# A two-layer trunk on one Trainium2 core: second shift and scale as whole matrix products on TensorE's column groups, and the convolution read from SBUF with two of its eight blocks on ScalarE and GpSimd

## The chip, the core and the metric

One core of one Trainium2 chip runs the whole program. The metric is device microseconds of one execution, median of three runs. TensorE is called PE, VectorE DVE, ScalarE ACT, GpSimd POOL, SyncE SP.

## What is computed

256 tokens of 2048 features pass through two layers. A conditioning vector `c` gives, for each layer, six vectors of 2048: shift, scale and gate for the mixer, shift, scale and gate for the MLP.

```python
c_act = silu(c)
for l in range(2):
    mod = c_act @ ada_w[l] + ada_b[l]              # [2048] @ [2048, 12288]
    shift1, scale1, gate1, shift2, scale2, gate2 = split(mod, 6)
    h = rms(x, norm1_g[l]) * (1 + scale1) + shift1
    mix = even_mixer(h) if l % 2 == 0 else attention(h)
    x = x + gate1 * mix
    h = rms(x, norm2_g[l]) * (1 + scale2) + shift2
    x = x + gate2 * (square(relu(h @ mlp_w1[l])) @ mlp_w2[l])
```

The even mixer projects h to u, v, a, g (1024 columns each). Mixer A gates gelu(u) with a causal 128-token mix of gelu(v). Mixer B takes y = a * sigmoid(g), a causal depthwise convolution of 31 taps over the 256 tokens for each of 1024 channels, a LayerNorm over channels and silu. Both go side by side into one output projection `ab_w_out`. Everything is float32.

## The kernel before

Weights come from HBM in tiles of 1 MiB, each 512 rows of K by 512 columns (or, for conditioning, 128 rows by 2048 columns). SP issues these loads in one queue, in program order, into a ring of four buffers, `raw` (`wraw`, L111); the input projection's tiles go into the three `wh` buffers instead. Products are done in one of two ways:

- The even mixer's input projection is in plain float32 (`gemm32`, L144): per weight tile eight matmuls of 128x128 stationary and 128x512 moving. There are 32 such tiles, 12 in the four quarters at the start and 20 after them.
- All else is split into a high and a low part (`wtile`, L124; the split is ACT's L94 and DVE's L95) and takes three fast matmuls for one (L183 to L185): 24 per tile. The output projection has 16 tiles, the MLP of a layer 128.

The scale and shift of the mixer and of the MLP are needed with features on the partitions ("columns"), the gates the same in every partition ("rows"). Either is a product of one vector with a 16 MiB matrix, and before the change DVE does nearly all of it: each weight is multiplied by its c and added to an accumulator of 128 partitions, and only the 128 partial sums go through PE. The work is cut into steps of one 1 MiB weight load each, kept in a queue (`ada_more`) and released by `side_work` (L134), so many steps per weight tile of the main products.

In the even mixer, from the point where `setup_even` is called:

- The row of gate 1 (`ada_row(0, 2)`, 16 steps and a finish) goes by ACT, which multiplies, and POOL, which adds (L302, L303).
- The columns of shift 2 and scale 2 (indices 3 and 4) go in quarters of 512 features (`ada_quarters(0, 3)`, 32 steps; L267, L269). The first quarter, 8 steps, is shared by ACT and POOL (L263, L265), the other three, 24 steps, are DVE's. The rates are 1.2, 2.5 and 0.8 steps per weight tile, so that the last steps run beside the first MLP tiles. `norm_start` needs only a quarter to be complete before the MLP's features of that quarter are made.
- The convolution is 8 blocks of 128 channels by 31 taps. Each block's padded input is copied to a PSUM bank (`yp`, L537), and every tap is one DVE instruction on 128x256 that reads that bank and the sum in SBUF (L540, L542). Ten taps are issued per weight tile, the rest before `layer_norm`.
- The output projection starts three of its four column chunks with mixer A's rows (six tiles; the third chunk's sums lie in the two `ms` banks) before mixer B's rows, which need `layer_norm`, enter.

A tile framework orders the instructions of each engine from this program; each engine then runs its own list in order, and waits at an instruction whose inputs are not there.

The lines that the prediction names: L153 the float32 matmuls, L183 to L185 and L210 to L212 the split ones, L94 and L95 the split, L107 transposes, L263, L265, L267, L269 the quarters, L302 and L303 gate 1, L297 the second layer-0 gate on DVE, L540 and L542 the taps, L607 and L616 the sums of `layer_norm`, L796 and L797 scores of the odd layer.

Of the kernel before, what the change touches and what calls it, by code (L numbers as in the profile page):

```python
# [36 lines left out]
R0, R1, R2, R4 = 1.2, 0.8, 0.75, 0.4  # L37
RA, NA = 2.5, 4
# [4 lines left out]
class Trunk:  # L43
    def __init__(self, ctx, tc, t):
# [12 lines left out]
        self.ms = pool("ms", 2, space=bass.MemoryType.PSUM)  # L57
# [4 lines left out]
        self.first = 0  # tiles still to be split by GpSimd  # L62
        self.conv_rate = 10
        self.conv_y = {}
        self.quarters = {}

# [1 line left out]
    def rsqrt(self, out, v):  # L68
        """out = v ** -0.5 for v > 0: a first guess from the bits, a third-order step, a Newton step."""
# [14 lines left out]
        # out <- 8/3 of its third-order step, then Newton with the 8/3 taken out again  # L84
# [7 lines left out]
    def split(self, src, hi, lo, engine=None):  # L92
        """src = hi + lo, both with the 12 significant bits that one pass of the array takes."""
        self.nc.scalar.copy(hi, src)  # L94
        (engine or self.nc.vector).tensor_tensor(lo, src, hi.bitcast(F32), op=ALU.subtract)  # L95
# [6 lines left out]
    def transpose4(self, srcs):  # L102
        """Up to four [128, n] blocks -> one PSUM bank, transposed side by side."""
        ps = self.tr.tile([P, 512], F32, tag="tr", name="trp")
        for i, s in enumerate(srcs):
            w = s.shape[-1]
            self.nc.tensor.transpose(ps[:w, i * P : i * P + s.shape[0]], s, self.ident[: s.shape[0], : s.shape[0]])  # L107
        return ps

# [14 lines left out]
    def wtile(self, w, k0, nk, n0, nw):  # L124
# [3 lines left out]
        # VectorE is busy with the norm when a phase's first tiles come: GpSimd splits those  # L128
# [6 lines left out]
    def side_work(self, size=1.0):  # L135
        """Work that is spread beside the weight tiles: conditioning and the convolution."""
# [7 lines left out]
        for _ in range(min(self.conv_rate, len(self.conv_queue))):  # L144
            self.conv_queue.pop(0)()
# [79 lines left out]
    def ada_col(self, layer, j):  # L225
        """self.mod[layer, j] = [128, 16], feature-major."""
# [19 lines left out]
    def ada_quarters(self, layer, j0, side=None, aided=0):  # L246
        """Columns j0 and j0 + 1 side by side, complete for 512 features after every eight steps.
        The first aided quarters go by ScalarE and GpSimd, with room for products in side."""
# [3 lines left out]
        def step(q, g, i):  # L252
# [6 lines left out]
            for k in range(4):  # L259
                c = self.cT[:, 4 * g + k : 4 * g + k + 1]  # L260
                if q < aided:
                    prod = acc if g + k == 0 else side[:, D + k * 512 : D + (k + 1) * 512]
                    nc.scalar.activation(prod, raw[:, k, :], AF.Copy, scale=c)  # L263
                    if g + k:
                        nc.gpsimd.tensor_tensor(acc, acc, prod, op=ALU.add)  # L265
                elif g + k == 0:
# [11 lines left out]
    def ada_row(self, layer, j, side=None):  # L278
        """self.mod[layer, j] = [128, 2048], the same in every partition. With side = [128, 4096],
        the products go to ScalarE and the sums to GpSimd."""  # L280
# [3 lines left out]
        def step(kb):  # L284
            raw = self.wraw(self.t["ada_w"][layer], kb, 1, j * D, D)
            if kb == 0:
                if side is None:
                    acc = self.tmp.tile([P, D], F32, tag="acc", name="acc", bufs=1)
                else:
                    acc = side[:, :D]  # L290
                box["acc"] = acc
# [6 lines left out]
            else:  # L298
                for i in range(2):
                    sl = slice(i * 1024, (i + 1) * 1024)  # L300
                    prod = side[:, D + i * 1024 : D + (i + 1) * 1024]
# [16 lines left out]
    def at_end(self, last):  # L318
        """Before the last product of a stage: no more work beside it."""
# [3 lines left out]
    def ada_more(self, rate, *lists):  # L323
        """Steps to be worked off beside the coming weight tiles, rate steps to a tile."""
# [26 lines left out]
    def norm_t(self, h, q, r):  # L351
        """Four blocks of (x * r).T in PSUM."""
# [4 lines left out]
    def norm_start(self, layer, which):  # L357
        """A function that gives 512 features' (shift, gain) columns: modulate(rms(x) * g) = x * rstd * gain + shift."""
# [14 lines left out]
    def norm_quarter(self, quarter, q, pair):  # L373
        """512 features of h.T, as (hi, lo)."""
# [10 lines left out]
    def norm_mod(self, layer, which):  # L385
        """h.T (hi, lo) of modulate(rms(x) * g, shift, scale)."""
# [6 lines left out]
    def gated(self, src, gate, h, c):  # L393
        """x[:, chunk] += gate * src, for one half"""
# [6 lines left out]
    def residual(self, ps, gate, c, last, part=None):  # L401
        """x[:, chunk] += gate * (ps + part)"""
# [621 lines left out]
```

## Time and profile before

| | |
|---|---|
| three runs | 2189.92, 2189.74, 2189.75 us; median 2189.75 |
| the profiled execution, first to last instruction | 2185.9 us |
| PE busy | 2090.9 us, 96% |
| DVE, ACT, POOL busy | 1564.9, 932.3, 146.7 us |
| bytes moved | 567.70 MB, mean 260 GB/s |
| granted PE clock, mean | 0.987 |

The profile is of one execution; its own time is not given apart, but the three runs lie 3.8 to 4.0 us above its span, and that much is taken to lie around the span. Times in the profile count from the first instruction. Busy PE is not PE at its peak: matmuls overlap, their ends are modelled, and the clock can be granted at less than full speed; so beside the busy time one reads how many matmuls start in a stretch, and the granted clock. Engines that are late matter only where PE waits for them.

### The profile page before, as it was taken

The page shows a single profiled execution, that of the slowest core. Times are in us where ns is not written, and L with a number is a line of the kernel's source. Part 1 is how long each engine was busy: PE and PEld are TensorE (multiplying, and loading weights), DVE is VectorE, ACT ScalarE, POOL GpSimd, SP SyncE. Part 2 cuts the span into 40 slices and gives each one's busy share as a digit, 9 for nine tenths or more (in the row PEclk, how much of TensorE's full clock was granted, in tenths as well). Part 3 has the DMA queues.
Part 4 walks back from the last instruction along what each step waited for, and adds up shares of the span by engine and source line. Part 5 has one row for each costly group of instructions (what it writes and reads, how often), then busy time and mean ns, then how long its engine had stood idle before and what let it go on. Part 6 is the DMA issues. An engine that isn't in the chain of part 4 may idle for free.

```text
span 2185.9 us, 23655 instructions
## 1 busy us (share of the span) xinstructions
PE 2090.9 (96%) x9138; PEld 1635.7 (75%) x9138; DVE 1564.9 (72%) x1763; ACT 932.3 (43%) x1184; POOL 146.7 (7%) x95
## 2 busy tenths in 40 slices
PE   2889999899999999999998999989999999999999
PEld 1444458678888888888888787868888888888887
DVE  6849999888777878787767878766656545554555
ACT  2135435444444334333436776444434433433432
POOL 0038710000000000000001000010000000000000
PEclk9999999899999999999999999989999999999999
DMA  9999968899898899989755646647778556556653
GB/s 350 384 346 330 332 242 295 275 317 339 315 337 315 329 326 319 339 304 334 270 174 174 211 158 214 229 154 250 256 271 264 178 192 189 189 192 192 189 191 122
DMA packets 238620, 567.70 MB, mean 260 GB/s; under 512 B 9150, under 2 KB 17784, under 8 KB 221864
## 3 DMA queue, kind: packets, MB, share of 16 engines
q1 hardware_dynamic: 236288, 562.60, 74.3%
q10 hardware_dynamic: 1564, 2.28, 0.3%
q8 instruction: 72, 1.18, 0.2%
q0 software_dynamic: 656, 1.31, 0.2%
q14 instruction: 40, 0.33, 0.0%
HBM read 564.06 MB, written 2.10 MB: 259 GB/s over the span
## 4 chain that ended last, share of the span: by engine, by line
PE 85%; DVE 9%; DMA 5%; ACT 1%; issue 1%; SPq 0%; ACTq 0%; DVEq 0%
PE mm L183 23%; PE mm L184 23%; PE mm L185 23%; PE mm L153 4%; DMA raw<-in_ada_w 4%; PE trp L107 3%; DVE accq L269 2%; DVE cvsq L542 1%; DVE wl L95 1%; PE mm L210 1%; PE mm L211 1%; PE mm L212 1%; PE sc L797 1%; PE sc L796 1%; DMA raw<-in_mlp_w 1%
## 5 line engine op out<-in xcount | busy, mean ns | idle before, releaser
L95 DVE TENSOR_TENSOR wl<-raw,wh 128x2048 fp32r<-128x2048 f32 (+2 forms) x312 | 704.7, 2259 | 424.0 <-PE mm L184 317.9
L94 ACT CAST wh<-raw 128x2048 fp32r<-128x2048 f32 (+3 forms) x316 | 596.6, 1888 | 774.1 <-PE mm L185 515.2
L183 PE MATMUL mm<-wh,f_h 128*128 128x512 f32 x1024 | 399.6, 390 | 0.0
L185 PE MATMUL mm<-wh,f_l 128*128 128x512 f32 x1024 | 399.3, 390 | 0.0
L184 PE MATMUL mm<-wl,f_h 128*128 128x512 f32 x1024 | 398.7, 389 | 0.0
L185 PE MATMUL mm<-wh,h_l 128*128 128x512 f32 (+2 forms) x928 | 358.2, 386 | 0.0
L183 PE MATMUL mm<-wh,h_h 128*128 128x512 f32 (+2 forms) x928 | 358.2, 386 | 0.0
L184 PE MATMUL mm<-wl,h_h 128*128 128x512 f32 (+2 forms) x928 | 357.0, 385 | 0.6 <-DVE wl L95 0.6
L185 PEld LDWEIGHTS mm<-wh,f_l 128*128 128x128 f32 x1024 | 192.2, 188 | 39.8
L184 PEld LDWEIGHTS mm<-wl,f_h 128*128 128x128 f32 x1024 | 192.3, 188 | 39.6
L183 PEld LDWEIGHTS mm<-wh,f_h 128*128 128x128 f32 x1024 | 192.3, 188 | 39.2
L184 PEld LDWEIGHTS mm<-wl,h_h 128*128 128x128 f32 x928 | 175.0, 189 | 34.0 <-DVE wl L95 1.1
L185 PEld LDWEIGHTS mm<-wh,h_l 128*128 128x128 f32 x928 | 174.9, 188 | 33.4
L183 PEld LDWEIGHTS mm<-wh,h_h 128*128 128x128 f32 x928 | 175.0, 189 | 32.7
L153 PE MATMUL mm<-raw,x 128*128 128x512 f32 x448 | 195.7, 596 | 1.0 <-ACT x L500 0.6
L269 DVE SCALAR_TENSOR_TENSOR accq<-raw,cT,accq 128x512 f32<-128x512 f32 x210 | 153.7, 749 | 16.6 <-DMA raw<-in_ada_w 13.3
L153 PEld LDWEIGHTS mm<-raw,x 128*128 128x128 f32 x448 | 84.6, 191 | 104.6 <-issue 98.5
L237 DVE SCALAR_TENSOR_TENSOR acc<-raw,cT,acc 128x2048 f32<-128x2048 f32 x60 | 140.8, 2346 | 9.7 <-DMA raw<-in_ada_w 9.7
L297 DVE SCALAR_TENSOR_TENSOR acc<-raw,cT,acc 128x2048 f32<-128x2048 f32 x48 | 112.7, 2347 | 4.4 <-DMA raw<-in_ada_w 4.4
L542 DVE SCALAR_TENSOR_TENSOR cvsq<-yp,convw,cvsq 128x256 f32<-128x256 f32 x240 | 96.0, 476 | 0.0
L303 POOL TENSOR_TENSOR side<-side 128x1024 f32<-128x1024 f32 x32 | 74.8, 2361 | 19.3 <-ACT side L302 19.3
L452 ACT ACTIVATE relu<-mm 128x512 f32<-128x512 f32 x60 | 35.8, 599 | 87.7 <-PE mm L185 81.5
(270 smaller groups left out, 2246.9 us busy)
## 6 DMA issues: line engine op xcount, KB each, us to landing
raw<-in_mlp_w SPq DMA_DIRECT2D x256, 1024.0 KB, 5.6
raw<-in_ada_w SPq DMA_DIRECT2D x192, 1024.0 KB, 5.4
raw<-in_ab_w_in SPq DMA_DIRECT2D x32, 1024.0 KB, 9.7
raw<-in_ab_w_out SPq DMA_DIRECT2D x16, 1024.0 KB, 8.3
raw<-in_mla_w_out SPq DMA_DIRECT2D x16, 1024.0 KB, 4.9
raw<-in_mla_w_ukv SPq DMA_DIRECT2D x8, 1024.0 KB
raw<-in_mla_w_uq SPq DMA_DIRECT2D x8, 768.0 KB, 4.8
raw<-in_mla_w_in SPq DMA_DIRECT2D x4, 1024.0 KB, 7.2
```

Of the source, the lines that this page charges most:

```text
L94: self.nc.scalar.copy(hi, src)
L95: (engine or self.nc.vector).tensor_tensor(lo, src, hi.bitcast(F32), op=ALU.subtract)
L107: self.nc.tensor.transpose(ps[:w, i * P : i * P + s.shape[0]], s, self.ident[: s.shape[0], : s.shape[0]])
L153: self.nc.tensor.matmul(ps[h], x[:, 4 * g + k, h * P : (h + 1) * P], raw[:, k, :], start=g + k == 0, stop=4 * g + k == KB - 1,)
L183: nc.tensor.matmul(o, a, hi[:, i, :nw], start=first, stop=False)
L184: nc.tensor.matmul(o, a, lo[:, i, :nw], start=False, stop=False)
L185: nc.tensor.matmul(o, b, hi[:, i, :nw], start=False, stop=last)
L237: nc.vector.scalar_tensor_tensor(acc, raw, self.cT[:, kb : kb + 1], acc, op0=ALU.mult, op1=ALU.add)
L269: self.last = nc.vector.scalar_tensor_tensor(acc, raw[:, k, :], c, acc, op0=ALU.mult, op1=ALU.add).ins
L297: nc.vector.scalar_tensor_tensor(acc, raw, c, acc, op0=ALU.mult, op1=ALU.add)
L303: nc.gpsimd.tensor_tensor(acc[:, sl], acc[:, sl], prod, op=ALU.add)
L542: nc.vector.scalar_tensor_tensor(o, y, wk, o, op0=ALU.mult, op1=ALU.add)
```

## The change

Four things are changed in the even mixer of layer 0; the rest of the program is the same but for names of PSUM buffers.

1. Shift 2 and scale 2 are no longer done in quarters. A new function, `ada_col_pe`, takes each 1 MiB step (128 rows of K by 2048 columns) as four float32 matmuls on PE. The stationary operand is one column of c, repeated 32 times; each matmul takes 512 of the 2048 columns as its moving operand and writes 32 partitions of one PSUM bank, `ms1`, so that the four lie in the four groups of 32 columns of the array. After 16 steps a copy on ACT and 16 small matmuls turn the four rows into columns with the bias.
2. The order: gate 1's steps alternate with those of shift 2, then come scale 2's, 49 steps in all at 1.5 per weight tile (`RB`). Nothing of it is left for the MLP.
3. The convolution: taps read the padded input in SBUF, and DVE's sums lie in PSUM (`ms0`, two blocks in one bank). Blocks 6 and 7 go by ACT, which multiplies both blocks' 128x256, and POOL, which adds 128x512 (`aided`). Eight DVE taps and two aided ones are issued per weight tile.
4. The `ms` banks being taken, the output projection starts two chunks with mixer A's rows (four tiles), not three.

```diff
-R0, R1, R2, R4 = 1.2, 0.8, 0.75, 0.4
-RA, NA = 2.5, 4
+RA, RB, R2, R4 = 8 / 3, 1.5, 0.75, 0.4
...
+    def ada_col_pe(self, layer, j):
...
+        def step(kb):
+            raw = self.wraw(self.t["ada_w"][layer], kb, 1, j * D, D)
+            if kb == 0:
+                box["acc"] = self.bank(1)
+            acc = box["acc"]
+            for s in range(4):
+                nc.tensor.matmul(
+                    acc[32 * s : 32 * s + 32], self.cT[:, kb : kb + 1].broadcast_to([P, 32]),
+                    raw[:, s * 512 : (s + 1) * 512], start=kb == 0, stop=kb == KB - 1,
+                )
+            if kb == KB - 1:
+                rows = self.tmp.tile([P, 512], F32, tag="t512", name="adar")
+                nc.scalar.copy(rows, acc)
...
+                for b in range(4):
+                    o = ps[:, 4 * b : 4 * b + 4]
+                    nc.tensor.matmul(o, rows[:, b * P : (b + 1) * P], firsts, start=True, stop=False)
+                    nc.tensor.matmul(o, self.ident, bias[:, b], start=False, stop=True)
...
-        g1, q34 = self.ada_row(layer, 2, side), self.ada_quarters(layer, 3, side, 1)
...
-        self.ada_more(R0, mixed)
-        self.ada_more(RA, q34[:NA])
-        self.ada_more(R1, q34[NA:])
+        g1 = self.ada_row(layer, 2, sq.rearrange("p a b -> p (a b)"))
+        s2 = self.ada_col_pe(layer, 3) + self.ada_col_pe(layer, 4)
+        mixed = [step for two in zip(g1[:16], s2) for step in two] + [g1[16]] + s2[16:]
+        self.ada_more(RB, mixed)
...
-                if k == 0:
-                    self.conv_y[b] = self.ms.tile([P, PAD + T], F32, tag="ms", name="yp")
-                    nc.scalar.copy(self.conv_y[b], ypad[:, b, :])
-                o, y, wk = cv[:, b, :], self.conv_y[b][:, k : k + T], self.convw[:, b, k : k + 1]
+                if k == 0 and b % 2 == 0:
+                    self.conv_acc[b // 2] = self.bank(0, (P, 2, T))
+                i, y, wk = self.conv_acc[b // 2][:, b % 2], ypad[:, b, k : k + T], self.convw[:, b, k : k + 1]
+                o = i if k < CONV_W - 1 else cv[:, b, :]
...
+            def aided(b, k):
+                prod = cv[:, b : b + 2, :] if k == 0 else self.tmp.tile([P, 2, T], F32, tag="t512", name="cvp")
+                for i in range(2):
+                    y, wk = ypad[:, b + i, k : k + T], self.convw[:, b + i, k : k + 1]
+                    if k == 0:
+                        nc.scalar.activation(prod[:, i], y, AF.Identity, bias=self.vecs[:, 64 + b + i : 65 + b + i], scale=wk)
+                    else:
+                        nc.scalar.activation(prod[:, i], y, AF.Copy, scale=wk)
+                if k:
+                    nc.gpsimd.tensor_tensor(cv[:, b : b + 2, :], cv[:, b : b + 2, :], prod, op=ALU.add)
...
+        self.conv_queue = [([], 8), ([], 2)]
...
-        pss = [self.psum2(), self.psum2(), [self.ms.tile([P, 512], F32, tag="ms", name=f"ms{h}") for h in range(NH)]]
+        pss = [self.psum2(), self.psum2()]
...
-            if c < 3:
+            if c < 2:
```

How this moves instructions, at three places. In the rows below, `raw`, `wh` and `wl` are weight buffers, `x0` the features, `cT` the columns of c, `mm` and `ms` PSUM banks, `trp` a bank for transposes; numbers tell one buffer from another; lines are those of the kernel that the row is from, L161 being L153 of before, L191 to L193 being L183 to L185, and L102 being L95.

PE's list in the last part of the input projection (the products of v and u), before:

```order
L153 MATMUL mm0_1151<-raw_1239,x0_117 128x512 x4
L153 MATMUL mm1_1152<-raw_1239,x0_117 128x512 x4
L107 MATMUL trp_1287<-ident_88,accq_762 128x128 x4
L153 MATMUL mm0_1273<-raw_1275,x0_117 128x512 x4
L153 MATMUL mm1_1274<-raw_1275,x0_117 128x512 x4
L153 MATMUL mm0_1273<-raw_1312,x0_117 128x512 x4
L153 MATMUL mm1_1274<-raw_1312,x0_117 128x512 x4
```

And in the changed kernel, in the same part:

```order
L291 MATMUL ms1_734<-raw_1191,cT_98 32x512 x4
L161 MATMUL mm0_1181<-raw_1183,x0_117 128x512 x4
L161 MATMUL mm1_1182<-raw_1183,x0_117 128x512 x4
L161 MATMUL mm0_1181<-raw_1221,x0_117 128x512 x4
L161 MATMUL mm1_1182<-raw_1221,x0_117 128x512 x4
L291 MATMUL ms1_734<-raw_1255,cT_98 32x512 x4
L161 MATMUL mm0_1181<-raw_1253,x0_117 128x512 x4
L161 MATMUL mm1_1182<-raw_1253,x0_117 128x512 x4
```

Before, PE's list holds nothing of a conditioning step but four transposes when a quarter ends; now a group of four L291 stands ahead of most weight tiles. In all there are 128 of them, in 34 unbroken runs, most of four, some of one, three or eight.

DVE's list where the input projection ends and the first output weights are split, before (`accq` are sums of the quarters, `mod_763` and `mod_764` finished columns):

```order
L542 SCALAR_TENSOR_TENSOR cvsq<-yp,convw,cvsq 128x256 x34
L95 TENSOR_TENSOR wl<-raw,wh 128x2048
L267 TENSOR_SCALAR accq<-raw,cT 128x512 x2
L269 SCALAR_TENSOR_TENSOR accq<-raw,cT,accq 128x512 x3
L221 TENSOR_REDUCE mod_764<-trp 128x4
L269 SCALAR_TENSOR_TENSOR accq<-raw,cT,accq 128x512
L223 TENSOR_TENSOR mod_764<-mod_764,ada_b 128x4
```

And in the changed kernel (`vu` holds v and u, `pm` the mixed v, `cat` the output projection's input):

```order
L615 SCALAR_TENSOR_TENSOR vu_852<-vu_852,rv_1153,sgug_672 128x128 x16
L566 SCALAR_TENSOR_TENSOR ms0_1303<-ypad_240,convw_647,ms0_1303 128x256 x16
L566 SCALAR_TENSOR_TENSOR cvsq_242<-ypad_240,convw_647,ms0_1303 128x256 x2
L102 TENSOR_TENSOR wl_1674<-raw_1671,wh_1673 128x2048
L635 SCALAR_TENSOR_TENSOR vu_852<-pm_1468,vecs_183,vu_852 128x128 x4
L102 TENSOR_TENSOR cat_l_1467<-trp_1477,cat_h_1466 128x4x128
```

After the norm of v (L615) 18 taps are left, where before 69 stood between it and the first split, and no conditioning step follows the split.

PE's list in the output projection where mixer A's rows of the second chunk end, before:

```order
L184 MATMUL mm1_1509<-wl_1740,cat_h_1440 128x512
L185 MATMUL mm1_1509<-wh_1739,cat_l_1441 128x512
L107 MATMUL trp_1792<-ident_88,accq_762 128x128 x4
L183 MATMUL ms0_1510<-wh_1782,cat_h_1440 128x512
L184 MATMUL ms0_1510<-wl_1783,cat_h_1440 128x512
```

And in the changed kernel:

```order
L192 MATMUL mm1_1535<-wl_1795,cat_h_1466 128x512
L193 MATMUL mm1_1535<-wh_1794,cat_l_1467 128x512
L291 MATMUL ms1_1679<-raw_1834,cT_98 32x512 x4
L291 MATMUL ms1_1679<-raw_1840,cT_98 32x512 x4
L191 MATMUL mm0_1532<-wh_1830,cat_h_1466 128x512
```

Before, a third chunk's two tiles of mixer A follow (into `ms0` and `ms1`); now two conditioning steps follow and then the first tile of mixer B's rows, into `mm0_1532`, the bank of chunk one.

More of the change, by code (lines that the diff above doesn't have):

```diff
@@ L62, in __init__, with bank, next_bank @@
         self.first = 0
-        self.conv_rate = 10
-        self.conv_y = {}
+        self.conv_acc = {}
+        self.turn = 0
         self.quarters = {}
+    def bank(self, i, shape=(P, 512)):
+        return self.ms.tile(list(shape), F32, tag=f"ms{i}", name=f"ms{i}")
+    def next_bank(self, shape=(P, 512)):
+        self.turn ^= 1
+        return self.bank(self.turn, shape)
     def rsqrt(self, out, v):
@@ L143, in side_work @@
             self.ada_queue.pop(0)[1]()
-        for _ in range(min(self.conv_rate, len(self.conv_queue))):
-            self.conv_queue.pop(0)()
+        for queue, rate in self.conv_queue:
+            for _ in range(min(rate, len(queue))):
+                queue.pop(0)()
     def gemm32(self, ps, x, w, g, n0):
@@ L244, in ada_col, with ada_quarters @@
         return [lambda kb=kb: step(kb) for kb in range(KB)]
-    def ada_quarters(self, layer, j0, side=None, aided=0):
+    def ada_quarters(self, layer, j0):
         nc = self.nc
@@ L260, in step @@
                 c = self.cT[:, 4 * g + k : 4 * g + k + 1]
[L261 to L266, printed above, removed]
+                if g + k == 0:
                     nc.vector.tensor_scalar(acc, raw[:, k, :], c, None, op0=ALU.mult)
@@ L276, in ada_quarters @@
         return [lambda q=q, g=g, i=i: step(q, g, i) for q in range(4) for g in range(4) for i in range(2)]
+    def ada_col_pe(self, layer, j):
+        nc = self.nc
+        box = {}
+        def step(kb):
[11 more added lines that the diff above has]
+                nc.scalar.copy(rows, acc)
+                ps = self.tr.tile([P, 512], F32, tag="tr", name="adac")
+                firsts = self.ident.rearrange("p (a b) -> p a b", b=32)[:, :, 0]
+                b0 = layer * 96 + j * KB
+                bias = self.ada_b[:, b0 : b0 + KB].rearrange("p (s b) -> p b s", b=4)
+                for b in range(4):
+                    o = ps[:, 4 * b : 4 * b + 4]
+                    nc.tensor.matmul(o, rows[:, b * P : (b + 1) * P], firsts, start=True, stop=False)
+                    nc.tensor.matmul(o, self.ident, bias[:, b], start=False, stop=True)
+                out = self.const.tile([P, KB], F32, tag=f"mod{layer}{j}", name=f"mod{layer}{j}")
+                nc.scalar.copy(out.rearrange("p (s b) -> p b s", b=4), ps[:, :KB].rearrange("p (b s) -> p b s", b=4))
+                self.mod[layer, j] = out
+        return [lambda kb=kb: step(kb) for kb in range(KB)]
     def ada_row(self, layer, j, side=None):
@@ L286, in step @@
             if kb == 0:
[L287 to L291, printed above, removed]
+                acc = box["acc"] = self.tmp.tile([P, D], F32, tag="acc", name="acc", bufs=1)
                 nc.gpsimd.memset(acc, 0.0)
@@ L427, in mlp @@
         self.hold = self.hold and layer > 0
-        started = [self.psum2(), self.psum2(), [self.ms.tile([P, 512], F32, tag="ms", name=f"ms{h}") for h in range(NH)]]
+        started = [self.psum2(), self.psum2(), [self.bank(h) for h in range(NH)]]
         for q in range(4 + AHEAD):
@@ L478, in even @@
         x = self.act.tile([P, KB, T], F32, tag="act", name="x0")
-        side = self.act.tile([P, 2 * D], F32, tag="act", name="side")
-        self.ada_more(8 / 3, self.ada_quarters(layer, 0))
+        self.ada_more(RA, self.ada_quarters(layer, 0))
         self.ada_steps(X_AT)
@@ L493, in even @@
         cv, sq = cvsq[:, 0], cvsq[:, 1]
-        pa, pg = self.psum2(), self.psum2()
-        pa1 = [self.ms.tile([P, 512], F32, tag="ms", name=f"pa1{h}") for h in range(NH)]
+        pa, pg, pa1 = self.psum2(), self.psum2(), [self.bank(h) for h in range(NH)]
         for q in range(4):
@@ L585, in even @@
                 )
-        self.ada_until(lambda: (layer, 2) in self.mod and self.quarters[layer, 3] >= 1)
         hh, hl = self.act_pair(KB, "cat")
@@ L822, in attend @@
             V = Vs[c % 3]
[L823 removed]
+            po = self.next_bank((P, 2, T))
             for i, pT in enumerate(pTs):
```

27 lines of the change are left out of this document (13 added, 14 removed).

## The prediction

> **What bounds the kernel now.** I read first the busy times of the engines on the page and the shares of the chain that ended last.
>
> ```profile
> PE 2090.9 (96%) x9138; PEld 1635.7 (75%) x9138; DVE 1564.9 (72%) x1763; ACT 932.3 (43%) x1184; POOL 146.7 (7%) x95
> PE 85%; DVE 9%; DMA 5%; ACT 1%; issue 1%; SPq 0%; ACTq 0%; DVEq 0%
> ```
>
> PE is the bound on the average. The change concerns one stretch, so the next view is the table by stretch: the last 20 input tiles (130 to 290), mixer A's end and the first output tiles (290 to 320), the output projection (to 410), the way into the MLP (to 430, with its first chunks to 510), and the MLP.
>
> ```profile
> core 0: us, PE busy (x) PEld busy (x) DVE busy (x) ACT busy (x) POOL busy (x), PEclk, DMA share, GB/s
> 130.00:290.00 160.00, 157.73 (x399) 71.51 (x400) 122.80 (x293) 80.66 (x108) 116.32 (x66) 1.00 0.90 325
> 290.00:320.00 30.00, 24.81 (x98) 16.99 (x97) 28.09 (x53) 9.10 (x12) 0.00 (x0) 0.83 0.66 230
> 320.00:410.00 90.00, 90.00 (x407) 74.30 (x406) 86.71 (x103) 40.67 (x41) 0.00 (x0) 1.00 0.85 297
> 410.00:430.00 20.00, 9.79 (x37) 7.49 (x36) 16.26 (x43) 9.14 (x19) 0.00 (x0) 0.66 0.79 263
> 430.00:510.00 80.00, 77.44 (x361) 62.68 (x360) 70.46 (x68) 36.80 (x45) 1.81 (x1) 1.00 0.86 294
> 510.00:1148.00 638.00, 638.00 (x2886) 527.33 (x2885) 493.41 (x319) 257.13 (x195) 4.36 (x6) 1.00 0.87 308
> ```
>
> In the columns of PE: it works 157.73 of 160 us, 90 of 90, 77.44 of 80 and 638 of 638, at full clock. What is put on PE's list in these stretches lengthens them, unless it falls into a hole; what is taken from DVE there gains only where PE waited for DVE. Counting also the part of the busy time that a clock below 1.00 took, the holes are:
>
> - 130 to 290: 160 - 157.73 = 2.3 us.
> - 290 to 320: 5.2 idle, and 24.81 x (1 - 0.83) = 4.2 by the clock, 9.4 us.
> - 410 to 430: 10.2 idle, and 9.79 x (1 - 0.66) = 3.3, 13.5 us.
> - 430 to 510: 2.6 us.
>
> In all 27.8 us, the most that relief of any other engine can return here. The chain of waits says whose the second hole is.
>
> ```profile
> 278.44 12.61 DVE cvsq L542 x33
> 291.05 0.24 issue
> 291.30 0.47 DVE cvsq L542
> 291.77 2.19 DVE wl L95
> 294.00 5.03 DMA raw<-in_ab_w_out
> 299.20 1.90 ACT wh L94
> 301.10 0.98 ACT vu L583 x2
> ```
>
> DVE works off its late taps until 291.8, only then splits the first output tile; that frees a `raw` buffer, the next load takes it, and ACT's cast of that load (L94) stands ahead of the gelu (L583) that mixer A's gate is made from.
>
> All sums below are differences to this execution's span of 2185.9 us; with the 3.85 us around it that is the median, 2189.75. A measurement of this kernel can tell about 0.2%, 4.4 us, from no change.
>
> **What is put on PE.** Thirty-two steps of four float32 matmuls, 128 in all, each with 512 moving columns. The kernel's other whole float32 matmuls give the price: the chain's one unbroken stretch of them, and the groups of L153's matmuls and weight loads.
>
> ```profile
> 188.17 53.23 PE mm L153 x124
> ```
>
> ```profile
> L153 PE MATMUL mm<-raw,x 128*128 128x512 f32 x448 | 195.7, 596 | 1.0 <-ACT x L500 0.6 <-DMA raw<-in_ab_w_in 0.4
> L153 PE MATMUL pa<-raw,x 128*128 128x512 f32 x64 | 32.0, 654 | 7.1 <-DMA raw<-in_ab_w_in 7.1
> L153 PEld LDWEIGHTS mm<-raw,x 128*128 128x128 f32 x448 | 84.6, 191 | 104.6 <-issue 98.5
> ```
>
> The program has 32 tiles x 8 = 256 such matmuls and the trace 448 + 64 = 512 records: each float32 matmul is two records. One record takes 53.23 / 124 = 0.429 us of PE. The moving columns are as many in L291, so its 256 records cost 0.429 each, if they run by themselves; that only 32 columns of the array are used saves nothing by this row. What matters is how many run at once, and no matmul of the kernel before uses column groups. So there are three cases.
>
> - One after another: 256 x 0.429 = 109.8 us, 3.4 per step of four.
> - Staggered: records start in the order of the list. A matmul's second record uses the columns of its first and waits for it; the next matmul's first record, in other columns, then runs beside that second one. A run of m matmuls takes m + 1 units in place of 2m. With 128 matmuls in 34 runs: (128 + 34) x 0.429 = 69.5 us.
> - Side by side: all four groups at once, two units for a run of four; with the longer and shorter runs of the list 74 units, 31.7 us.
>
> I take staggered, an estimate from the order alone: the list puts the two records of one matmul next to each other, and in every chain row here records run in the order of the list.
>
> The Trainium skill ("TensorE: Matmul & The Clock Gate", Part 3: Packing small matmuls — row/col tiling) says that matmuls whose outputs lie in different column groups run at the same time, and gives 2.38 times the speed for three of 512 columns; by that the third case holds, and the sum below would be 2225. The same section says that matmuls are "pc-monotone in start AND end — strict FIFO, no reordering"; with the two records of a float32 matmul in line, that speaks for the second case and 2270. No run here shows either.
>
> Each L291 also loads its own 32 weight columns. A load of 128 takes 0.191 us by the row above and lies under the matmul before it. In the staggered case the groups leave less cover; a quarter of 0.191 for a quarter of the columns is 0.05, and 128 x 0.05 = 6.4 us. Bounds: 0 (all hidden) and 128 x 0.191 = 24. The other two cases have cover enough or fill the array anyway; there I count 0.
>
> A change between whole-array and partial matmuls has a price too. The nearest rows are the scores of the odd layer, where a part of the array's rows is used (L797) in turn with the whole (L796).
>
> ```profile
> 1311.64 0.43 PE sc L796 x2
> 1312.07 0.63 PE sc L797 x2
> 1312.70 0.42 PE sc L796 x2
> 1313.12 0.41 PE sc L797 x2
> 1313.53 0.43 PE mm L183
> 1313.96 0.23 PE mm L184
> ```
>
> L797 takes 0.63 after an L796 of 0.43, and the first whole matmul after it takes 0.43 where the next takes 0.23: 0.20 us per switch. The list has 34 runs of L291 between whole matmuls: 34 x 2 x 0.20 = 13.6 us. Bounds 0 (hidden) and 13.6.
>
> Small matmuls: the quarters' 32 transposes go, and 16 small matmuls of two records come.
>
> ```profile
> 707.21 0.87 PE trp L107 x8
> ```
>
> A transpose is 0.11: 32 x 0.11 = 3.5 us off and 32 records x 0.11 = 3.5 on, net 0.
>
> **What is given back.** The hole at 290: in the new list DVE has 18 taps left after the norm of v where it had 69, so 51 taps x 0.382 (12.61 / 33) = 19 us of the backlog are gone, and the split comes in time. Late next are the norm of v and ACT's gelu, which stand in series; I take 7 of the 9.4 us, bounds 0 and 9.4. The 2.6 us after 430 come back too: no conditioning step is left there. The hole at 410 I leave: PE's rows of that stretch show its three waits.
>
> ```profile
> 410.79 0.39 PE L185 MATMUL mm<-wh,cat_l 128*128 128x512 f32 x1
> 419.13 1.08 PE L107 MATMUL trp<-ident,xn 128*128 128x128 f32 x4 [7.95 <-DVE nr L87]
> 422.48 0.80 PE L210 MATMUL mm<-wh,h_h 128*128 128x512 f32 x1 [2.26 <-DVE h_h L382]
> ```
>
> They are the serial residual, mean square, root, norm and modulation, which the change leaves; DVE's quarter steps between them give way to steps of the second gate, fewer and longer (L297, quoted below). Bounds 0 and 10. Back in all 7 + 2.6 = 9.6 us.
>
> **What is hidden.** The rows for the other engines:
>
> ```profile
> L542 DVE SCALAR_TENSOR_TENSOR cvsq<-yp,convw,cvsq 128x256 f32<-128x256 f32 x240 | 96.0, 476 | 0.0
> L269 DVE SCALAR_TENSOR_TENSOR accq<-raw,cT,accq 128x512 f32<-128x512 f32 x210 | 153.7, 749 | 16.6 <-DMA raw<-in_ada_w 13.3
> L297 DVE SCALAR_TENSOR_TENSOR acc<-raw,cT,acc 128x2048 f32<-128x2048 f32 x48 | 112.7, 2347 | 4.4 <-DMA raw<-in_ada_w 4.4
> L303 POOL TENSOR_TENSOR side<-side 128x1024 f32<-128x1024 f32 x32 | 74.8, 2361 | 19.3 <-ACT side L302 19.3
> ```
>
> ```profile
> L265 POOL TENSOR_TENSOR accq<-accq,side x30: 1262/1272/1832, 152.1 to 281.2; 128x512 f32<-128x512 f32 x30
> ```
>
> ```profile
> L624 ACT ACTIVATE cvsq<-cvsq,vecs x8: 587/590/602, 344.1 to 348.6; 128x256 f32<-128x256 f32 x8
> ```
>
> DVE loses 62 taps x 0.40 = 25 us and 24 steps x 4 x 0.73 (153.7 / 210) = 70 us; it is no bound between 130 and 290 (122.80 of 160) and less so after. Should its taps from SBUF be slower beside POOL, 178 of them could take 0.476 in place of 0.40, 14 us, less than it loses. ACT gains 62 products x 0.59 = 37 us and loses some 32 x 0.7, in a stretch where it works 80.66 of 160. POOL exchanges 30 additions of 1.27 for 30 of the same 128x512, and is still done after 116 of 160 us. Their cover is PE's dense list; without it they would cost at most ACT's net 15 us.
>
> SP's queue moves the steps from the MLP ahead to the input projection: 20 tiles and 33 steps there, 53 x 1.05 MB = 55.6 MB. The best rate that the trace shows is this one.
>
> ```profile
> 50.00:60.00 10.00, 10.00 (x25) 4.40 (x24) 9.68 (x15) 0.00 (x0) 0.00 (x0) 1.00 1.05 387
> ```
>
> At 387 GB/s that is 144 us, under PE's 157 before any addition: hidden. A `raw` buffer of a step now comes free only when PE reaches it, but PE's other work is what all wait for. That the MLP begins without steps of this layer gains nothing, as PE is dense there already.
>
> `layer_norm` gets four output tiles as cover, not six. It lasts from the first sum to the last split.
>
> ```profile
> L607 PE MATMUL stat<-cvsq,onesr x16: 379/379/381, 320.2 to 323.5; 128*128 128x256 f32 x16
> ```
>
> ```profile
> L269 DVE SCALAR_TENSOR_TENSOR accq<-raw,cT,accq x13: 743/747/753, 320.0 to 351.1; 128x512 f32<-128x512 f32 x13
> ```
>
> ```profile
> L95 DVE TENSOR_TENSOR cat_l<-cvsq,cat_h x2: 1218/1220/1221, 349.2 to 354.0; 128x1024 fp32r<-128x1024 f32 x2
> ```
>
> That is 34 us, with DVE's quarter steps in between; a tile of 24 matmuls at 0.227 (90.00 / 407 with the small ones, 0.23 in the rows at 1313) covers 5.4. Two tiles less are 10.9 us of cover less, against the 13 additions of quarter steps that DVE no longer has there (13 x 0.747 = 9.7 us) and the L291 runs, which are cover too. So 0, bounds 0 and 10.
>
> **The sum.** Staggered: 69.5 + 6.4 + 13.6 - 9.6 = +79.9, 2270 us.
>
> **The rivals.**
> - *Side by side*: 31.7 + 13.6 - 9.6 = +35.7, 2225. For it: separate columns and separate partitions of the bank; against it: two records per matmul in one list.
> - *One after another*: 109.8 + 13.6 - 9.6 = +113.8, 2304. For it: the stretch at 188 shows one record per 0.429 through 124 of them, and no row shows two that share the time of one.
> - *Faster: DVE's relief closes PE's holes.* If a run costs one record, 34 x 0.43 = 14.6 with nothing for switches, and all 27.8 us of holes close, it is -13, 2177. It decides when a run costs under 27.8 / 34 = 0.82 us, less than two records and their switches. The dense rows speak against it, the chain through DVE at 278 to 302 for a third of it.
> - *No change*: side by side, no price for switches, all holes closed: 31.7 - 27.8 = +4.
> - *A wait for `layer_norm`* adds up to 10 to any of these; its place is the fourth output tile, and it decides when norm and split take over 22 us and the L291 runs there.
>
> **How the numbers follow.** Staggered 0.45, one after another 0.20, side by side 0.25, faster 0.06, no change 0.04. The likeliest gives 2270; its own bounds are 2250 (no switches, no loads) to 2298 (loads of 24, and the norm's 10). The range takes in side by side without the price of switches, 2225 - 13.6 = 2212, and one after another with a little of the norm, 2308. Left out are faster, no change, and some tenths of the outer two cases, together under 0.2. Faster by over 0.2% 0.06, within 0.04, slower 0.90.
>
> **What would show it.** In the new profile an L291 run of four takes 5 x 0.43 + 4 x 0.05 + 0.4 = 2.7 us of the chain (staggered), 1.3 (side by side) or 3.8 (one after another). PE stays dense at 130 to 290, which becomes some 50 us longer, the output projection some 35; the slow clock near the end of the input projection is gone; DVE has more idle time; the MLP has its 638 us. I am wrong if a run costs under 1 us, if PE has new holes of over 10 us there, or if the stages after 510 us change.

## The result, and the profile after

The changed kernel takes 2216.68 us (median of four runs, 2214.32 to 2217.70) against 2189.74 us: 26.9 us slower, ratio 1.0122, 95% interval 1.0107 to 1.0136. The direction was forecast, the size was not: 80 us were forecast, a third of them came. The profiled execution spans 2212.6 us, 26.7 more than before.

The page of the changed kernel, busy times and the chain's shares:

```profile
PE 2126.6 (96%) x9394; PEld 1637.2 (74%) x9394; DVE 1508.8 (68%) x1589; ACT 936.2 (42%) x1210; POOL 145.7 (7%) x95
PE 91%; DVE 5%; DMA 4%; ACT 0%; issue 0%; SPq 0%; DVEq 0%; ACTq 0%
```

PE has 256 records more and 36 us more of work, and the chain runs through PE for 91% of the span in place of 85%. The table by stretch, cut near where the stages now lie (the input projection with mixer A's end, most of the output projection, its last tiles and the way into the MLP, the MLP's first chunks, the MLP):

```profile
core 0: us, PE busy (x) PEld busy (x) DVE busy (x) ACT busy (x) POOL busy (x), PEclk, DMA share, GB/s
155.80:331.00 175.20, 173.81 (x547) 72.60 (x547) 141.19 (x245) 78.75 (x122) 103.27 (x58) 1.00 0.86 322
331.00:420.00 89.00, 89.00 (x446) 62.73 (x445) 44.95 (x44) 37.29 (x41) 1.81 (x1) 1.00 0.78 281
420.00:454.00 34.00, 24.68 (x108) 19.89 (x108) 27.88 (x38) 13.97 (x17) 0.00 (x0) 0.92 0.82 284
454.00:540.00 86.00, 86.00 (x394) 71.01 (x395) 68.75 (x57) 42.41 (x54) 0.00 (x0) 0.97 0.81 272
540.00:1180.00 640.00, 639.56 (x2892) 528.12 (x2892) 480.52 (x317) 257.67 (x197) 7.06 (x7) 1.00 0.84 295
```

PE is dense through the input and the output projection at full clock; the hole that lay at 290 to 320 is gone. By marks that both programs have: the first output matmul comes at 323.6 in place of 310.4, the first MLP matmul (L210, now L218) at 454.0 in place of 422.5, and from there to the end it is 4.8 us less (1758.6 against 1763.4). So the change costs 13, then 18 more, and gives back 5.

The chain in the input projection shows what one step of four matmuls costs (columns: start, us, what; two records are one float32 matmul):

```profile
267.43 0.99 PE ms L291 x8
268.42 7.06 PE mm L161 x16
275.49 0.99 PE ms L291 x8
```

A step is 0.99 us, not 2.7. That is two units of 0.429 and 0.13 more. The 16 records behind it take 7.06 where 16 x 0.429 is 6.86, another 0.20 at their two ends. So a step costs 1.19: two units, and 0.33 for the change to narrow matmuls and back. All runs of L291, from their first record to the next other matmul, sum to 37.7 us in the trace; with 34 x 0.20 they are 44.5.

The records of one such step in stretches of time (columns: stretch, its length, then PE busy with the number of records that ran in it, PEld the same):

```profile
170.76:170.80 0.04, 0.03 (x4) 0.03 (x5) 1.00 0.98 410
170.80:171.20 0.40, 0.40 (x4) 0.12 (x8) 1.00 0.46 164
171.20:171.25 0.05, 0.05 (x8) 0.00 (x0) 1.00 0.77 328
```

Four records are under way within 0.04 us, and no other starts until 171.20, when the next four begin: in the trace their starts lie 0.007 us apart, and the second four follow 0.45 us after the first. These are two waves of four, one for each column group, and not a pair of records one behind the other.

DVE shows something that the prediction does not have. Ahead of mixer A's end stands the norm of v, 16 instructions of 128x128; this is its row in the kernel before and in the changed one (ns least, middle, most, then the first and the last start):

```profile
L575 DVE SCALAR_TENSOR_TENSOR vu<-vu,rv,sgug x16: 334/339/1416, 254.9 to 260.7; 128x128 f32<-128x128 f32 x16
```

```profile
L615 DVE SCALAR_TENSOR_TENSOR vu<-vu,rv,sgug x16: 340/1420/2451, 268.9 to 289.6; 128x128 f32<-128x128 f32 x16
```

The 16 took 6.2 us and take 21.1. POOL's timeline at that time:

```profile
265.91 13.41 POOL L578 TENSOR_TENSOR cvsq<-cvsq,cvp 128x512 f32<-128x512 f32 x10
279.28 9.49 POOL L333 TENSOR_TENSOR acc<-acc,cvsq 128x1024 f32<-128x1024 f32 x4
```

An addition of POOL takes 13.41 / 10 = 1.34 us with its gap, then 9.49 / 4 = 2.37; the norm's instructions go in step with them, at 1.42 and then 2.45 each, and are back at 0.34 when POOL stops at 288.8. Both of the norm's inputs lie in SBUF, as do POOL's. The taps, with one input in SBUF and the sum in PSUM, stay at 0.49. The Trainium skill ("SBUF — State Buffer", SBUF: two separate sides) says that a DVE instruction with two SBUF inputs and a GpSimd instruction that reads SBUF exclude each other, for the whole instruction, with the later one waiting. The trace agrees: twelve of the norm's instructions last until 0.15 us behind the end of an addition, and the four after POOL's last addition take 0.34. Which of two came first the rows don't tell.

### The profile page after: what moved, and what is told of

The parts are those of the page before. It is cut to its first block, busy times and chain, and to the rows that moved or that the text cites. A ratio compares the mean times of both kernels' runs of the same rounds, so it can differ in the third digit from the quotient of the medians.

```text
span 2212.6 us, 24008 instructions
## 1 busy us (share of the span) xinstructions
PE 2126.6 (96%) x9394; PEld 1637.2 (74%) x9394; DVE 1508.8 (68%) x1589; ACT 936.2 (42%) x1210; POOL 145.7 (7%) x95
## 3 DMA queue, kind: packets, MB, share of 16 engines
q0 software_dynamic: 656, 1.31, 0.2%
## 4 chain that ended last, share of the span: by engine, by line
PE 91%; DVE 5%; DMA 4%; ACT 0%; issue 0%; SPq 0%; DVEq 0%; ACTq 0%
PE mm L191 23%; PE mm L192 23%; PE mm L193 23%; PE mm L161 8%; PE trp L114 3%; DMA raw<-in_ada_w 3%; DVE accq L271 2%; PE ms L291 2%; PE mm L218 1%; PE mm L219 1%; PE mm L220 1%; PE ms L837 1%; PE ms L220 1%; PE ms L219 1%; PE ms L218 1%; DVE wl L102 1%
## 5 line engine op out<-in xcount | busy, mean ns | idle before, releaser
L102 DVE TENSOR_TENSOR wl<-raw,wh 128x2048 fp32r<-128x2048 f32 (+2 forms) x312 | 704.7, 2259 | 457.2 <-PE mm L192 322.8
L191 PE MATMUL mm<-wh,f_h 128*128 128x512 f32 x1024 | 399.6, 390 | 0.0
L193 PE MATMUL mm<-wh,f_l 128*128 128x512 f32 x1024 | 399.3, 390 | 0.0
L193 PE MATMUL mm<-wh,h_l 128*128 128x512 f32 (+2 forms) x928 | 358.4, 386 | 0.0
L191 PE MATMUL mm<-wh,h_h 128*128 128x512 f32 (+2 forms) x928 | 358.3, 386 | 0.0
L193 PEld LDWEIGHTS mm<-wh,f_l 128*128 128x128 f32 x1024 | 192.2, 188 | 40.0
L191 PEld LDWEIGHTS mm<-wh,f_h 128*128 128x128 f32 x1024 | 192.3, 188 | 39.3
L161 PE MATMUL mm<-raw,x 128*128 128x512 f32 x448 | 201.3, 605 | 1.1 <-ACT x L528 0.6
L193 PEld LDWEIGHTS mm<-wh,h_l 128*128 128x128 f32 x928 | 174.8, 188 | 33.4
L191 PEld LDWEIGHTS mm<-wh,h_h 128*128 128x128 f32 x928 | 175.1, 189 | 32.6
L161 PEld LDWEIGHTS mm<-raw,x 128*128 128x128 f32 x448 | 84.6, 193 | 114.2 <-issue 106.1
L271 DVE SCALAR_TENSOR_TENSOR accq<-raw,cT,accq 128x512 f32<-128x512 f32 x120 | 88.2, 750 | 14.8 <-DMA raw<-in_ada_w 12.2
L566 DVE SCALAR_TENSOR_TENSOR ms<-ypad,convw,ms 128x256 f32<-128x256 f32 x174 | 85.1, 489 | 5.5
L333 POOL TENSOR_TENSOR acc<-acc,cvsq 128x1024 f32<-128x1024 f32 x32 | 74.9, 2362 | 35.2 <-ACT cvsq L332 35.2
```

What stands on the lines that cost most here:

```text
L161: self.nc.tensor.matmul(ps[h], x[:, 4 * g + k, h * P : (h + 1) * P], raw[:, k, :], start=g + k == 0, stop=4 * g + k == KB - 1,)
L191: nc.tensor.matmul(o, a, hi[:, i, :nw], start=first, stop=False)
L193: nc.tensor.matmul(o, b, hi[:, i, :nw], start=False, stop=last)
L271: self.last = nc.vector.scalar_tensor_tensor(acc, raw[:, k, :], c, acc, op0=ALU.mult, op1=ALU.add).ins
L333: nc.gpsimd.tensor_tensor(acc[:, sl], acc[:, sl], prod, op=ALU.add)
L566: nc.vector.scalar_tensor_tensor(o, y, wk, i, op0=ALU.mult, op1=ALU.add)
```

## The experiments

The main theory after this profile: PE's list is the bound, and a step costs two waves and two switches. The main rivals: narrow matmuls are simply cheap; or the time is lost on something else, and the matmuls stand where PE would have waited. Each ratio is to the kernel before, measured beside it (medians of 2186.7 to 2188.2 us); its 95% interval stands in brackets.

**One column group.** Does the gain come from four groups at a time, or from 32 columns being cheap?

```diff
+            r = 32 * (kb % 4)
...
-                    acc[32 * s : 32 * s + 32], self.cT[:, kb : kb + 1].broadcast_to([P, 32]),
-                    raw[:, s * 512 : (s + 1) * 512], start=kb == 0, stop=kb == KB - 1,
+                    acc[r : r + 32], self.cT[:, kb : kb + 1].broadcast_to([P, 32]),
+                    raw[:, s * 512 : (s + 1) * 512], start=kb < 4 and s == 0, stop=kb >= KB - 4 and s == 3,
```

> The four matmuls of a step all go into one column group (another one for each step), so the sums of shift 2 and scale 2 come out mixed; number, shape and place of the instructions stay. Theory, side by side: the four groups of the array work at the same time, and a step in one group takes 8 records x 0.429 = 3.4 us and 0.2 for the way back to whole matmuls in place of 1.0 + 0.2; 32 x 2.4 = 78 more, about 2295 us. Rival, narrow matmuls are cheap: 32 columns take a quarter of the time by themselves, so nothing changes, 2217 us.

2283.09 us (one run), ratio 1.043. The chain has the step (L292 here) at

```profile
213.31 3.55 PE ms L292 x8
216.86 7.06 PE mm L161 x16
```

3.55 us, eight units of 0.429 and 0.12, in place of 0.99. All runs sum to 107.6 in place of 37.7 us: 69.9 us more in the trace, 66 more in time. The expected 78 were too many because a few steps that stand together, in different groups, do overlap. Groups run side by side; a narrow matmul alone is as long as a wide one.

**Steps in pairs, and in which order.** Loads of two steps, then their eight matmuls, either step by step (first `+for` line) or group by group (second). Gate 1's steps, with which they alternate, go by twos as well.

```diff
+            box[kb] = raw
+            if kb % 2 == 0:
+                return
-            for s in range(4):
+            for kk, s in [(kk, s) for kk in (kb - 1, kb) for s in range(4)]:
...
+            for kk, s in [(kk, s) for s in range(4) for kk in (kb - 1, kb)]:
...
-        mixed = [step for two in zip(g1[:16], s2) for step in two] + [g1[16]] + s2[16:]
+        mixed = [step for i in range(0, 16, 2) for step in g1[i : i + 2] + s2[i : i + 2]] + [g1[16]] + s2[16:]
```

> Two steps' eight matmuls stand together, step by step. Theory: the price of a run is whole waves of 0.429 and 0.33 for the two switches, so a pair takes 4 x 0.43 + 0.33 = 2.05 in place of 2 x 1.19; some 12 pairs are newly joined: 4 us less, 2213 us. Rival, the price goes by the matmul: 2217. Second rival, the buffer that is held longer starves the loads: over 2220.

> The same pairs, but group by group: both steps' matmul of the first group, then both of the second, and so on. Theory A, PE takes any later record whose columns are free: the same as the pairs step by step, about 2213. Theory B, records start strictly in the list's order, first parts of up to four matmuls ahead of their second parts: 9 waves for a pair in place of 4, 16 x 5 x 0.43 = 34 more, about 2247. Theory C, strictly in order with the two records of a matmul next to each other, as the prediction had it: 13 waves, 62 more, about 2275.

Step by step: 2210.15 us, ratio 1.0097 (1.0081 to 1.0114), 0.25% under the changed kernel's, 5 us; the two intervals just touch. Group by group: 2219.29 us (one run), ratio 1.014. A pair's 16 records in the chain of the one and of the other:

```profile
211.50 1.85 PE ms L294 x16
```

```profile
213.88 1.87 PE ms L294 x16
```

Four waves (4 x 0.43 + 0.13) in both. Group by group, two matmuls of one group stand next to each other in the program, and their records still do not hold up the other groups: theory A. The kernel's 9 us more than step by step are in part in its list: all its runs sum to 41.2 us in place of 36.1, as nine runs of a single matmul (0.98 us each) stand in it in place of four; the rest of this single run isn't placed. Whether PE itself passes over records or the list that it gets is in another order than the program isn't shown by these rows. One thing in the traces speaks for the first: the four starts of a wave lie 0.006 to 0.007 us apart step by step and nearly all 0.013 to 0.014 group by group, twice as far, as they would if PE went through twice as many records from one group to the next.

**Without the steps' matmuls.** If PE's list is the bound, leaving them out gives their price back.

```diff
-            for s in range(4):
+            for s in range(4 if kb == 0 else 0):
...
-                    raw[:, s * 512 : (s + 1) * 512], start=kb == 0, stop=kb == KB - 1,
+                    raw[:, s * 512 : (s + 1) * 512], start=True, stop=True,
```

> Leaves out 31 of 32 steps of L291 (each column's sum takes only the first step's four matmuls; 120 of 128 matmuls are gone); loads, copies and convolution stay. Theory: PE's list is the bound, a step costs 1.2 us, and DVE's relief has closed the holes that the steps stand in for; 2217 less 30 x 1.2 + some split runs, 38 in all: about 2179 us, under the kernel before. Rival, the time is lost elsewhere (the norm's thinner cover, the taps from SBUF): over 2195 us.

2206.25 us, ratio 1.0080 (1.0065 to 1.0095). Only 0.42%, some 9 us, of 38 came back, and the kernel without the work is still slower than before. The theory falls at this point. PE now waits, most of all here (PE's timeline, in brackets idle time and who ended it; then the stretch, with the columns of the table above):

```profile
303.72 0.74 PE L114 MATMUL trp<-ident,vu 128*128 128x128 f32 x2 [13.21 <-DVE vu L635]
```

```profile
290.00:320.00 30.00, 13.77 (x45) 7.32 (x43) 18.42 (x38) 6.78 (x10) 4.71 (x2) 0.71 0.25 93
```

13 us of waiting for DVE, and a clock of 0.71 in that stretch. DVE is late by its norm of v:

```profile
L615 DVE SCALAR_TENSOR_TENSOR vu<-vu,rv,sgug x16: 1147/1930/2443, 257.9 to 285.0; 128x128 f32<-128x128 f32 x16
```

It takes 29.5 us here, each instruction in step with a POOL addition. In the changed kernel the steps' matmuls cover it: PE has no such wait there.

**And without POOL's additions for the convolution.**

```diff
-                if k:
+                if k == 1:
                     nc.gpsimd.tensor_tensor(cv[:, b : b + 2, :], cv[:, b : b + 2, :], prod, op=ALU.add)
```

> As without the steps, and 29 of POOL's 30 additions of the convolution left out as well (the sums of two blocks lack their products). Theory, shared port: the norm of v is back near 6 to 12 us in place of 29, the hole of 13 us at 290 and the slow clock behind it go: 2185 to 2190. Rival, loads set the pace of that stage: within 3 us of the run without the steps, 2206.

2190.92 us, ratio 1.0013 (1.0004 to 1.0022): 15 us less. The norm is short again but for a few instructions:

```profile
L615 DVE SCALAR_TENSOR_TENSOR vu<-vu,rv,sgug x16: 338/339/2452, 248.0 to 256.2; 128x128 f32<-128x128 f32 x16
```

Without the steps' matmuls and the additions, it is still no faster than the kernel before. What is left lies in the output projection, where PE waits for splits that come late behind their loads (the stretch, then a load in the chain):

```profile
306.00:378.00 72.00, 67.42 (x307) 52.49 (x306) 40.56 (x47) 33.70 (x41) 1.81 (x1) 0.98 0.90 348
```

```profile
347.08 10.58 DMA raw<-in_ab_w_out
```

An output tile's load is 10.6 us of the chain, and the queue moves 348 GB/s.

**And without scale 2's loads.** The 49 steps all come ahead of the MLP, 14 of L291's beside the output tiles.

```diff
-            raw = self.wraw(self.t["ada_w"][layer], kb, 1, j * D, D)
+            if j == 3 or kb == 0:
+                raw = self.wraw(self.t["ada_w"][layer], kb, 1, j * D, D)
```

> As without the steps and the additions, and 15 of the 16 loads of scale 2 left out as well. Theory, loads are the next bound: the holes of 5 us and the slow clock between 354 and 385 close, because the output tiles no longer queue behind 14 steps' loads: 2179 to 2185. Rival: no change, 2191.

2182.07 us, ratio 0.9976 (0.9967 to 0.9985), as expected: the first kernel of this line that is faster than before. The stretch:

```profile
306.00:378.00 72.00, 69.85 (x318) 56.18 (x316) 44.57 (x45) 37.03 (x41) 1.82 (x1) 0.98 0.51 178
```

So three limits lie behind one another: PE's matmuls (9 us when they go first), POOL's additions against DVE (15), and the loads, or the `raw` buffers that they hold, which went with them (8). They were taken away in this order alone. In the changed kernel itself PE is busy 89.00 of 89 us beside the output tiles, so late loads cost nothing there, and what the additions alone cost there the next run shows. The last kernel keeps DVE's relief and leaves out nearly all that the change puts on PE and POOL, and scale 2's loads; ACT's products and shift 2's loads are still in it. It is only 5 us faster than before.

**One part of the change at a time.** The columns on PE with the whole convolution on DVE; and the new convolution with the quarters kept, all on DVE (a second difference, since ACT and POOL shared the first quarter before).

```diff
-                    if b == 6:
+                    if b == 8:
...
-        self.conv_queue = [([], 8), ([], 2)]
+        self.conv_queue = [([], 10), ([], 0)]
```

> The changed kernel with all eight blocks of the convolution on DVE: 62 more taps of 0.49 us, 30 us more for DVE, and POOL without its 30 additions. Theory, shared port: in the changed kernel the norm of v (L615) takes 25 us in place of 6 because each of its instructions lasts as long as a POOL addition, so most of what the two blocks save is lost again; without the additions it gets 10 to 20 us back and the time stays within 2214 to 2224. Rival, the two blocks are a real relief: DVE is 30 us later at the first split, of which the changed kernel has some 10 in hand: 2230 or more.

2214.40 us, ratio 1.0127 (1.0111 to 1.0142), the same as the whole change. The norm of v:

```profile
L615 DVE SCALAR_TENSOR_TENSOR vu<-vu,rv,sgug x16: 347/347/348, 262.1 to 266.1; 128x128 f32<-128x128 f32 x16
```

4.3 us in place of 21.1: 17 us of the 30 that two blocks save on DVE are lost to POOL's additions, the convolution's own and four of gate 1's. What is left moves nothing, since PE is the bound there: the loss of 27 us comes without the two blocks too.

```diff
-        g1, q34 = self.ada_row(layer, 2, side), self.ada_quarters(layer, 3, side, 1)
+        g1, q34 = self.ada_row(layer, 2, side), self.ada_quarters(layer, 3, side, 0)
```

(with the taps and the aided blocks of the changed kernel)

> The kernel before with the new convolution alone; shift 2 and scale 2 stay in quarters, now all four on DVE (8 steps, 23 us more for DVE, against 30 less of taps). Theory, shared port: POOL's additions now fall on the norm of v and on the quarter steps, 10 to 20 us; the hole at 298 gets longer: 2195 to 2205. Rival, no such price: DVE is 7 us earlier, 2183 to 2190.

2203.36 us, ratio 1.0083 (1.0066 to 1.0100). Slower too, and the hole is at another place than was expected:

```profile
285.16 1.12 PE L107 MATMUL trp<-ident,accq 128*128 128x128 f32 x4 [17.90 <-DVE accq L270]
```

PE stands 17.9 us at the transposes that end the first quarter, as this quarter, DVE's now, ends late, while PE's list has it in the middle of the input tiles. The shared port has a part in it, as was expected: on the chain ahead of this the norm of v takes 17.7 us, and quarter steps of 128x512 that take 0.66 without POOL take 2.37 beside its additions. How much is the port's and how much the eight more steps', this run does not separate, so it does not price the convolution by itself.

**Closing the hole of before without PE.** The hole of before (PE idle from 298, in the stretch of 290 to 320) looked cheap to close by DVE's order alone. Three edits of the kernel before:

```diff
-RA, NA = 2.5, 4
+RA, NA = 2.5, 0
```

> The kernel before with one number changed: the four quarter steps that stood at 2.5 a tile beside the last input tiles go at 0.8 as the others do. Theory: DVE is some 10 us earlier at the first output split, and most of the 10 us hole at 298 closes: 2180 to 2185. Rival: the same steps are then late at the start of the MLP, which waits: 2190 to 2200.

2207.56 us, ratio 1.0101 (1.0086 to 1.0116): the rival, and worse than its 2190 to 2200. The quarter that was put off is waited for by PE's transposes beside the MLP:

```profile
466.49 1.09 PE L107 MATMUL trp<-ident,accq 128*128 128x128 f32 x4 [5.49 <-DVE accq L269]
```

```diff
-            if c == 0:
-                while self.conv_queue:
-                    self.conv_queue.pop(0)()
-                layer_norm()
             for g in (0, 4):
                 self.gemm_part(ps, cat, 0, wo, 0, g, KB, c * 512, 512)
+            if c == 0:
+                while self.conv_queue:
+                    self.conv_queue.pop(0)()
+                layer_norm()
```

> The kernel before with one edit: the last taps and the norm over channels are issued behind the first two output tiles, not ahead of them, so that DVE's first split stands ahead of the taps' end. Theory: the hole at 298 needs no relief by PE, only another place in DVE's list; most of its 10 us close and the cover of two tiles less costs little: 2178 to 2183. Rival: the norm over channels comes late and PE waits at mixer B's rows: 2187 or more.

2188.38 us, ratio 1.0009 (1.0000 to 1.0018): the rival's time. And the third:

```diff
+            if c == 0:
+                self.first = 2
```

> The kernel before, with POOL making the low parts of the first two output tiles in place of DVE, as the kernel lets it do elsewhere. Theory: POOL is free from 282 on, so the first split is ready before 290 and the hole at 298 closes by 5 to 10 us: 2178 to 2183. Rival: POOL's subtraction takes as long as DVE's backlog, or shuts DVE out of SBUF meanwhile: 2187 or more.

2189.96 us, ratio 1.0011 (1.0002 to 1.0019). The second and the third edit gain nothing. The hole stays, at one of gate 1's last matmuls, in the second and in the third:

```profile
306.19 0.79 PE L312 MATMUL gps<-gl,onesr 128*128 128x512 f32 x1 [5.28 <-DVE gl L95]
```

```profile
308.86 0.79 PE L312 MATMUL gps<-gl,onesr 128*128 128x512 f32 x1 [8.38 <-DVE gl L95]
```

In both chains quarter steps stand ahead of gate 1's split (gl) now, which PE waits for (a row of the second edit's chain, then two of the third's):

```profile
294.19 2.65 DVE accq L269 x4
```

```profile
297.06 4.43 DVE mod L223
...
306.00 1.43 DVE accq L269 x2
```

Taps or splits that are moved away let quarter steps in at their place: the hole is made of DVE's work up to there, not of one split's place. In the third edit the port has a part in it, as its rival said: L223, an addition of 128x4, took 4.43 us of the chain and ended with POOL's second low part (5.09 us, 296.38 to 301.47).

**The two better variants together**: pairs, and the convolution on DVE.

> The changed kernel with both improvements seen so far: steps in pairs (6.5 us less) and all eight blocks of the convolution on DVE (2 us less). Theory: PE's list is the bound, so the pairs' gain stays whole and that of the blocks is PE's small part: 2206 to 2211. Rival: with less on PE's list, DVE's 62 additional taps come to light: 2214 or more.

2211.38 us, ratio 1.0109 (1.0095 to 1.0123), at the upper end of what was expected: no better than the pairs alone (1.0097). No version here, with all its work in it, beats the kernel before.

## Why the prediction was right or wrong

- **Slower, because PE is dense and gets more work**: right, and the profile after shows it. All of the work was taken to be felt, and on PE's dense list it is; but without the matmuls the kernel is only 9 us faster and still slower than before, as other limits lie close behind, which the prediction counted as hidden.
- **69.5 us for the records, staggered**: wrong, and the step that failed. "The list puts the two records of one matmul next to each other" was argued, not seen; the trace shows the first records of four matmuls together and then the second ones. Two units a step, 0.99 us, as in the rival of 0.25. The forecast's 69.5 + 6.4 + 13.6 = 89.5 us for L291 measured 44.5. The time lies within the range all the same, because the range was stretched at its low end to take in the side-by-side case; that says nothing for the mechanism that was chosen. By the runs, in-order stagger isn't there even where the program puts two matmuls of one group next to each other.
- **6.4 us for weight loads**: nothing. Loads of 32 columns take 0.108 us, about half of a whole load's 0.191 and not the quarter that was estimated, but the waves follow each other at 0.43 and hide them.
- **13.6 us for switches**: 0.33 a run in place of 0.40, 34 x 0.33 = 11.2. The term is about right.
- **The side-by-side rival's 31.7 + 13.6 = 45.3**: the trace has 44.5. Its time of 2225 is 8 us above the measured one: 5 by what came back beyond the 9.6, the rest by these 0.8 and by what is not placed below.
- **7 us back at the hole of 290**: it is gone whole; idle 4.42 and 0.68 us and 10.2 us at half clock made it 10. **2.6 us back after 430**: 4.8. Eight transposes of a quarter stood there (0.9 us), which the prediction had counted as net nothing; the rest of the difference isn't placed.
- **The hole at 410 stays**: right. Its longest wait is 7.12 in place of 7.95 us.

```profile
450.69 1.11 PE L114 MATMUL trp<-ident,xn 128*128 128x128 f32 x4 [7.12 <-DVE xn L384]
```

- **`layer_norm` has cover enough**: right; PE is busy 89.00 of 89 us there.
- **DVE, ACT, POOL and loads are hidden**: right in the sum, since PE covers them, but by less than was thought. DVE's price of POOL's additions was looked for at the taps (14 us) and lies at the norm of v (17 us of DVE's time, 15 of the kernel's once PE no longer covers it); the loads were checked against the best rate for the input projection alone, and it is the output projection where they are short once PE has less to do.
- **What would show it**: of the signs that were named, PE's density and the end of the slow clock came. The input projection was to become some 50 us longer and the output projection 35; from mark to mark they became 13 and 19 longer (the output matmuls start from 310.4 to 410.8 us before, from 323.6 to 443.2 after). A run of four was to take 2.7 us and takes 1.19, near the 1.3 that the prediction gave for side by side; its own row of 0.99 is just under the 1 us that was named as a sign of being wrong.

With 44.5 for L291, some 10 back at the hole and 5 after 430, the sum is +29 to 30; measured are 26.7. Of the 44.5, 1.4 us are no matmul's: inside one run PE waits 1.39 us for DVE's L553, and the kernel before waits 1.31 at the same work (L529). Without them the sum is +28, and some 1.5 us are not placed.

## What to carry to other kernels

Before pricing work by the number of records, ask how many can run at once, and where no row shows their order, do not let an argued order choose the value: price each order, and ask which row would tell them apart. A dense engine hides the next limit: leave the added work out, then what shows up behind it, and so on, before calling the work the cause; here each of three layers, taken away in turn, was worth 8 to 15 us. When work goes to GpSimd, look for DVE instructions with both inputs in SBUF at the same time, for they pay the addition's whole length.

## What the runs showed of the hardware

- Four float32 matmuls of 32 stationary columns in different column groups take 0.99 us, in the same group 3.55 us: 3.6 times.
- Going from whole to 32-column matmuls and back costs 0.33 us in all: 0.13 within the run of narrow ones (0.99 against 2 x 0.429) and 0.20 in the whole ones beside it (7.06 against 16 x 0.429).
- A 128x128 DVE instruction with two SBUF inputs takes 0.34 us alone, 1.42 beside POOL additions of 1.27 and 2.45 beside those of 2.4.
